# Projection weights' low parts moved to VectorE in halves, the next tile's rounding moved behind the ended tile's copies, and seven dummy matmuls added to the first norm

## The chip, the core and the metric

The program runs on one core of one Trainium2 chip. TensorE (PE) multiplies, VectorE (DVE) and ScalarE (ACT) do the work on rows, GpSimd (POOL) does some elementwise work and issues DMAs, and SyncE (SP) issues most loads. The metric is the device time in microseconds (us) of one execution, the median of several.

## What is computed

One layer of a transformer for 128 context tokens and 512 latent tokens, width 1024, in fp32. Cut to what matters here:

```python
h = rmsnorm(x, n1) * (1 + sc1) + sh1
aq, ak, av, bq, bk, bv, ga, gb = split(h @ w_in)      # 34 tiles of 128 columns
a_o = block_attention(aq, ak, av)                     # mixer A: 8 query heads, 2 key heads
b_o = neighbourhood_attention(bq, bk, bv, rel_bias)   # mixer B: 8 heads, window on the grid
m = sigmoid(ga) * (a_o @ w_br_a) + sigmoid(gb) * (b_o @ w_br_b)
x = x + g1 * (m @ w_out)
x = x + g2 * (square(relu(h2 @ w_mlp_in)) @ w_mlp_out)
y = rmsnorm(x, final_g)
```

The shifts, scales and gates come from `silu(c) @ w_mod + b_mod`.

## The kernel before

**Three products for one.** Every large product is made of three: an operand is split into a high part, rounded to the matmul's format, and a low part, what the rounding left off. PE adds high*high, high*low and low*high into one PSUM bank (`gemm_k`, lines 310 to 312). So each tile of weights needs a rounding on ACT (`wh`, line 263) and a subtraction `wl = wst - wh` (line 269 on POOL, line 271 on DVE), or, for the tiles in `LOSET`, a negated copy on ACT and a DMA that adds the weights to it (lines 265 and 266).

**The stages.** The first stage (0 to 52 us) makes the norm, the modulation and the first three tiles of the projection; its order is written out by hand (`manual_schedule`, from line 431), and `warm(n)` in it issues n dummy matmuls of 128x128 on PE. Then comes the attention (52 to 345 us): for mixer A and then mixer B, a head's scores (`S`, lines 672 and 725), softmax, transposes (`T`, lines 682 and 742), the split of the transposed rows into `ph` on ACT and `pl` on DVE (lines 620 and 621), and the product with the values into `po` (lines 689 and 690, 753 and 754). `combine` (lines 627 and 628) takes `po` away. Between these steps the Filler puts the matmuls of the remaining tiles of the projection on PE, 48 of them for one tile, two halves of 24, each half into a bank `pg`. In mixer A there is one `pg` bank, so the next half starts when the last half's copy (`raw`, `kr` or `qs`, lines 857 to 861 and 564, 565) has emptied it. After 345 us come the gates, the output projection and the MLP.

**Whose turn it is.** In the attention a scheduler orders each engine's instructions by the place at which the program issues them and by estimated times; each engine then runs its own row in order, and waits at the head of it. `fill_tile` (line 825) issues one tile's matmuls and copies. When a tile's last matmul is issued, `W.done()` (line 843) frees its weights and calls `conv` for the tile three places on: ACT's rounding in two halves, then the low part. The staging buffer `wst` (3 of them) is free for the next load on SP once the low part is made.

**Queries.** `a_q_rot` (line 817) turns a query tile by its position (`rope`: lines 554 to 557 on DVE), then `qa_part` splits it for the two heads e = 0 and 1: ACT copies (line 570), and a subtraction (line 571) on POOL or DVE by a bit of `QP`.

Of the kernel before, what the change touches and what calls it, by code (L numbers as in the profile page):

```python
# [19 lines left out]
KT = 8  # L20
EPS = 1e-6
FIRST = (4, 0, 5)
AFILL = (21, 29, 1, 10, 2, 6, 3, 14, 22)
BFILL = (30, 11, 7, 15, 12, 8, 16, 13, 9, 17)
# [3 lines left out]
WPO = 4  # L28
WP1 = 0
# [10 lines left out]
LAG = (0, 4)  # L40
MAN = (0,)
NSMALL = 348
QP = 3
Q0P = 0
RL = 1
OU = 1800
MG = 2
W2P = 2
WARM = (15, 1, 2, 5, 0, 2, 2)
NMS = 9  # L50
W0P = 0
WAH = (4, 6)
# [17 lines left out]
def trunk_layer(ctx: ExitStack, tc: tile.TileContext, xT, small_in, wmodA, wmodB, tabs, cacheK, cacheV, bias,  # L70
# [68 lines left out]
    def r32(ap):  # L139
        return ap.bitcast(F32)  # L140
# [94 lines left out]
    class Weights:  # L235
# [15 lines left out]
        def conv(self):  # L251
            self.feed()
            key, src = self.order[self.nc]
            self.busy -= 1
            st = self.st.pop(key)
            if key in EXTRA:
                self.extra = True
                hi, lo = (dp.tile([P, KT, P], F32R, tag="w4" + x, bufs=1, name="w4") for x in "hl")
            else:
                hi, lo = (wp.tile([P, KT, P], F32R, tag="w" + x, bufs=3, name="w" + x) for x in "hl")  # L260
                self.live += 2
            for ks in (slice(0, 4), slice(4, KT)) if key[0] == "in" else (slice(0, KT),):
                ACT.activation(hi[:, ks], st[:, ks], AF.Copy)  # L263
            if key in LOSET:
                ACT.activation(lo, r32(hi), AF.Copy, scale=-1.0)
                nc.gpsimd.dma_start(lo, src.bitcast(F32R).rearrange("p (k n) -> p k n", k=KT), accum_op=OP.add)
            elif key in WPOOLSET:
                for ks in (slice(0, 4), slice(4, KT)) if key[0] == "in" else (slice(0, KT),):
                    nc.gpsimd.tensor_sub(lo[:, ks], st[:, ks], r32(hi[:, ks]))  # L269
            else:  # L270
                DVE.tensor_sub(lo, st, r32(hi))
            self.t[self.nc] = (hi, lo)
            self.nc += 1

# [23 lines left out]
                OPS[0].ahead()  # L298

    OPS = []  # L300
    WPOOLSET = {("in", n) for n in AFILL + BFILL} | {("out", n) for n in range(WPO, KT)} | {("w1", n) for n in range(WP1)}
    EXTRA = {("out", 4), ("w1", 0)}
    LOSET = {(x, n) for x, a, b in LOACC for n in range(a, b) if x != "in" or n not in GATES[2:]}
    W = Weights()
# [50 lines left out]
    def mod_product(f, q):  # L355

        for k in range(4):
            g = 32 * k
            PE.matmul(pm[f % 2][g:g + 2, :256], sc_e[:, 4 * q + k], MS[f, q][:, k * 256:(k + 1) * 256],
                      start=q == 0, stop=q == 1, tile_position=(0, g))  # L360
# [70 lines left out]
    with tc.manual_schedule(engines={e.engine for e in (PE, ACT, DVE, nc.gpsimd, nc.sync)}):  # L431
        for f in range(2, KT):
            mod_load(f)
            if f % 2 == 0:
                w0_load(f // 2)
        for p in pm:
            DVE.memset(p[:, :256], 0.0)
        ACT.activation(sc_e, cc, AF.Exp, scale=-1.0)
        DVE.tensor_scalar(sc_e, sc_e, 1.0, None, op0=OP.add)
        DVE.reciprocal(sc_e, sc_e)  # L440
        DVE.tensor_mul(sc_e, sc_e, cc)
        DVE.tensor_scalar(b1, bm, 1.0, None, op0=OP.add)
        warm(WARM[0])
        for i in range(3):
            squares(i)
            warm(WARM[i + 1])
        mod_product(0, 0)
        squares(3)
        mod_product(0, 1)
        mod_rows(0, DVE)  # L450
        for h, sl in enumerate(HALVES):
            ACT.activation(rstd[:, sl], mean[h][:, :HT], AF.Ln, bias=eps)
        for h, sl in enumerate(HALVES):
            ACT.activation(rstd[:, sl], rstd[:, sl], AF.Exp, scale=-0.5)
        warm(WARM[4])
        mod_cols(0)
        warm(WARM[5])
        h_scaled(0)
        w0_conv(0, (0, 1), "h")
        w0_conv(0, (0,), "l")  # L460
        h_hi(0, SEG0)
        mod_product(1, 0)
        w0_conv(0, (2,), "h")
        w0_conv(0, (1, 2), "l")
        first_gemm(0, 0, 0)
        mod_product(1, 1)
        mod_rows(1)
        h_lo(0)
        first_gemm(0, 1, 0)
        mod_cols(1)  # L470
        h_scaled(1)
        first_gemm(0, 2, 0)
        h_hi(1)
        for i in range(3):
            first_gemm(0, i, 1)
        for q in range(2):
            mod_product(2, q)
        mod_rows(2)
        h_lo(1)
        w0_conv(1)  # L480
        for f in range(1, KT - 1):
            if f + 2 < KT:
                first_gemm(f, 0, 0)
            mod_cols(f + 1)
            h_scaled(f + 1)
            if f + 2 < KT:
                mod_product(f + 2, 0)
            else:
                first_gemm(f, 0, 0)
            first_gemm(f, 1, 0)  # L490
            if f + 2 < KT:
                mod_product(f + 2, 1)
            h_hi(f + 1)
            if f + 2 < KT:
                mod_rows(f + 2)
            first_gemm(f, 2, 0)
            for i in range(3):
                first_gemm(f, i, 1)
            h_lo(f + 1)
            if f % 2 == 0 and f < KT - 2:  # L500
                w0_conv(f // 2 + 1)
            if f == 3:
                silu_rows()
            if f in WAH:
                W.conv()
        for i in LASTO:
            for part in range(2):
                first_gemm(KT - 1, i, part)
# [316 lines left out]
    def fill_tile(n, F):  # L825
# [7 lines left out]
        for h in range(2):  # L833
            sl = HALVES[h]
            pg = ps_g()
            ps = pg[:, :HT]
            for k in range(KT):
                gemm_k(ps, w, H1, h, k, k, k == 0, k == KT - 1)
                if k == 3:
                    F.flush(1)  # L840
                yield UNIT
            if h == 1:
                W.done()
            if kind == "bq":
                if h == 0:
                    qs = [qs_tile() for _ in range(2)]
                for e in range(2):
                    q_part(qs[e], e, sl, ps)
            else:
                if h == 0:  # L850
                    raw = kr_tile() if kind == "bk" else o_tile("raw")
                    if kind == "bk":
                        for c in (P, 6 * P):
                            DQ[QO].dma_start(raw[:, c:c + P], cacheK[:, (j + 1) * P:(j + 2) * P])
                if kind == "bk":
                    lat = slice(max(sl.start, P), sl.stop)
                    if h == 0:
                        ACT.activation(raw[:, 0:P], ps[:, 0:P], AF.Copy)
                    ACT.activation(raw[:, lat.start + P:lat.stop + P], ps[:, lat.start - sl.start:], AF.Copy)
                else:  # L860
                    ACT.activation(raw[:, sl], ps, AF.Copy)
            F.flush(1)
            yield 0
        F.flush()
# [875 lines left out]
```

## Time and profile before

| | before |
|---|---|
| median of 3 runs | 943.21 us (939.26 to 946.52) |
| the profiled execution's own time | 939.48 us |
| its span, first to last instruction | 937.6 us |
| PE busy | 914.2 us (98%) |
| PE weight loads busy | 878.5 us (94%) |
| DVE busy | 700.8 us (75%) |
| ACT busy | 566.8 us (60%) |
| POOL busy | 242.4 us (26%) |

The profile shows one execution. Busy time of PE is modelled at its ends, so a stall shorter than a matmul's tail does not appear as idle time; the weight loads, which run just ahead, show it better. What counts is which wait ends last at the places where PE stands.

### The profile page before, as it was taken

To read this page: it belongs to the slowest core of one execution; us is meant where nothing else is said; L and a number is where in the kernel's file an instruction comes from. 1 tells how busy PE (TensorE), PEld (TensorE's weight loads), DVE (VectorE), ACT (ScalarE), POOL (GpSimd) and SP (SyncE) were. 2 spreads that over 40 slices of the span, in tenths; PEclk is the share of its full clock that TensorE was granted. 3 is DMA by queue.
4 is the path that set the end of the run, shared out by engine and by line. 5 is a ranking of instruction groups with operands and counts; after the bars stand their busy time and mean duration, and the time that the engine had idled before them with its cause. 6 is when DMAs were issued, how large, how long until landed. Compare 5 with 4: busy or idle time off the path is not lost.

```text
span 937.6 us, 16618 instructions
## 1 busy us (share of the span) xinstructions
PE 914.2 (98%) x6152; PEld 878.5 (94%) x6152; DVE 700.8 (75%) x1451; ACT 566.8 (60%) x1153; POOL 242.4 (26%) x260
## 2 busy tenths in 40 slices
PE   8999899999999999999999999999999999999996
PEld 6799789889999899999999999999999999999995
DVE  5774776756556788576778996986699768975898
ACT  3566677757656785675433667536763566447765
POOL 0042421314331011211120010444233532364130
PEclk9999999999999999999999999999999999999998
DMA  9783310026355379989743471888769877798573
GB/s 346 277 239 121 87 46 26 23 74 169 106 145 135 113 207 301 257 235 288 232 158 123 112 192 58 151 188 191 169 128 193 173 162 168 158 182 188 100 114 112
DMA packets 54033, 151.08 MB, mean 161 GB/s; under 512 B 6657, under 2 KB 10385, under 8 KB 53953
## 3 DMA queue, kind: packets, MB, share of 16 engines
q1 hardware_dynamic: 31440, 100.27, 32.5%
q0 software_dynamic: 21360, 48.45, 29.5%
q10 hardware_dynamic: 1152, 1.31, 0.4%
q8 instruction: 48, 0.79, 0.3%
q14 instruction: 33, 0.26, 0.1%
HBM read 138.72 MB, written 4.60 MB: 153 GB/s over the span
## 4 chain that ended last, share of the span: by engine, by line
PE 76%; DVE 10%; DMA 4%; issue 4%; ACT 4%; POOL 2%; SPq 0%; DVEq 0%; POOLq 0%; ACTq 0%
PE b L1609 9%; PE b L1610 9%; PE b L1608 9%; PE pg L310 6%; PE pg L312 6%; PE pg L311 6%; PE pss L312 3%; PE pss L311 3%; PE pss L310 3%; PE pt L312 2%; PE pt L311 2%; PE pt L310 2%; DMA wsb<-w 2%; PE pss L401 1%; PE pt L682 1%
## 5 line engine op out<-in xcount | busy, mean ns | idle before, releaser
L1355 ACT ACTIVATE wb<-wsb 128x512 fp32r<-128x512 f32 x140 | 87.1, 628 | 93.8 <-PE b L1610 60.9
L1609 PE MATMUL b<-op,wb 128*128 128x320 f32 x448 | 138.7, 310 | 1.0 <-DVE op L1424 1.0
L1608 PE MATMUL b<-op,wb 128*128 128x320 f32 x448 | 138.6, 309 | 0.2 <-ACT op L1423 0.2
L1610 PE MATMUL b<-op,wb 128*128 128x320 f32 x448 | 138.4, 309 | 0.0
L1356 DVE TENSOR_TENSOR wb<-wsb,wb 128x512 fp32r<-128x512 f32 x128 | 93.6, 735 | 32.3 <-ACT wb L1355 32.2
L1359 POOL DMA_DIRECT2D wsb<-w x84 | 73.5, 921 | 128.8 <-DVE wb L1356 95.0
L263 ACT ACTIVATE wh<-wst 128x512 fp32r<-128x512 f32 (+1 forms) x84 | 59.7, 737 | 46.1 <-PE pg L311 16.5
L1609 PEld LDWEIGHTS b<-op,wb 128*128 128x128 f32 x448 | 84.1, 188 | 1.8 <-DVE op L1424 1.8
L1608 PEld LDWEIGHTS b<-op,wb 128*128 128x128 f32 x448 | 84.1, 188 | 0.7 <-ACT op L1423 0.5
L1610 PEld LDWEIGHTS b<-op,wb 128*128 128x128 f32 x448 | 84.1, 188 | 0.0
L1063 DVE SCALAR_TENSOR_TENSOR mt<-wmt,cb 128x512 f32<-128x512 f32 x128 | 80.7, 687 | 4.5 <-DMA wmt<-wmodB 4.5
L269 POOL TENSOR_TENSOR wl<-wst,wh 128x512 fp32r<-128x512 f32 (+1 forms) x37 | 52.6, 1437 | 118.7 <-ACT wh L263 109.9
L621 DVE TENSOR_TENSOR pl<-pt,ph 128x512 fp32r<-128x512 f32 (+2 forms) x80 | 50.9, 636 | 35.1 <-ACT ph L620 30.5
L1340 POOL DMA_DIRECT2D wsb<-w x28 | 26.7, 954 | 138.3 <-DMA wsb<-w 43.1
L620 ACT ACTIVATE ph<-pt 128x512 fp32r<-128x512 f32 (+2 forms) x80 | 44.2, 553 | 21.8 <-PE pt L682 10.3
L1467 DVE SCALAR_TENSOR_TENSOR x<-b,parts,x 128x128 f32<-128x128 f32 (+1 forms) x116 | 46.8, 435 | 3.0 <-PE b L1610 2.2
L1608 PE MATMUL b<-t,wb 128*128 128x320 f32 x144 | 44.7, 310 | 0.5 <-DVE tp L1453 0.5
L1355 ACT ACTIVATE wb<-wst 128x512 fp32r<-128x512 f32 x56 | 34.8, 625 | 16.3 <-PE b L1610 9.7
L1610 PE MATMUL b<-t,wb 128*128 128x320 f32 x144 | 44.5, 309 | 0.0
L1609 PE MATMUL b<-t,wb 128*128 128x320 f32 x144 | 44.5, 309 | 0.0
L1424 DVE TENSOR_TENSOR op<-hid,op 128x1280 fp32r<-128x1280 f32 (+2 forms) x32 | 37.0, 1156 | 7.8 <-ACT op L1423 7.7
L1467 DVE SCALAR_TENSOR_TENSOR x<-tp,parts,x 128x320 f32<-128x320 f32 (+2 forms) x60 | 38.7, 673 | 1.0 <-ACT tp L1512 1.0
(874 smaller groups left out, 3037.4 us busy)
## 6 DMA issues: line engine op xcount, KB each, us to landing
wsb<-w POOLq DMA_DIRECT2D x112, 256.0 KB, 5.3
wst<-w SPq DMA_DIRECT2D x36, 512.0 KB, 4.0
wmt<-wmodB SPq DMA_DIRECT2D x32, 512.0 KB, 5.4
wst<-w_in SPq DMA_DIRECT2D x31, 512.0 KB, 4.1
wsb<-w SPq DMA_DIRECT2D x28, 512.0 KB, 4.2
ms<-wmodA SPq DMA_DIRECT2D x16, 512.0 KB, 8.0
wl<-w_in POOLq DMA_DIRECT2D x11, 512.0 KB, 8.2
bt<-bias SPq DMA_DIRECT2D x16, 320.0 KB, 6.1
```

The source lines that it names most:

```text
L263: ACT.activation(hi[:, ks], st[:, ks], AF.Copy)
L310: PE.matmul(ps, wh[:, k], xh[:, sl], start=first, stop=False)
L311: PE.matmul(ps, wh[:, k], xl[:, sl], start=False, stop=False)
L312: PE.matmul(ps, wl[:, k], xh[:, sl], start=False, stop=last)
L1063: DVE.scalar_tensor_tensor(t, st[:, q * 512:(q + 1) * 512], 1.0, r32(cb[2 * q + i][:, :512]), op0=OP.mult, op1=OP.mult, accum_out=parts[:, ...
L1355: ACT.activation(w[:, 0:4], t, AF.Copy)
L1356: (nc.gpsimd if o in BLKPOOL[l - 1] else DVE).tensor_sub(w[:, 4:8], t, r32(w[:, 0:4]))
L1359: nc.gpsimd.dma_start(t, self.src(l, c, n, e)[:, 4 * half:4 * half + 4], accum_op=OP.add)
L1467: DVE.scalar_tensor_tensor(X1[i][:, sl], src[:, sl.start - off:sl.stop - off], g[:, j:j + 1], X1[i][:, sl], op0=OP.mult, op1=OP.add)
L1608: PE.matmul(b, w[:, k], xh, start=not whole and k == 0, stop=False, skip_group_check=True)
L1609: PE.matmul(b, w[:, k], xl, start=False, stop=False, skip_group_check=True)
L1610: PE.matmul(b, w[:, 4 + k], xh, start=False, stop=o not in ("A11", "S2", "S1") and k == 3, skip_group_check=True)
```

## The change

Four edits. (1) `WPOOLSET` loses its tiles of the projection, so the 17 of them that are not in `LOSET` have `wl` made on DVE, in two halves of 128x512 each, instead of on POOL in the same halves; the three projection tiles that were on DVE already (18, 19 and 26) are made in halves too. (2) `QP` goes from 3 to 2: of the six `qa_part` subtractions of query tiles 1 to 3, the three for e = 0 go from POOL to DVE. (3) `W.done()` stands behind the copies of the tile that ended and no longer ahead of them. (4) `WARM` has two more dummies behind the first squares, two ahead of the first `mod_cols`, and three, with a new call, behind the product that follows the first `h_hi`.

```diff
-QP = 3
+QP = 2
-WARM = (15, 1, 2, 5, 0, 2, 2)
+WARM = (15, 3, 2, 5, 2, 2, 3)
@@ Weights.conv
             else:
-                DVE.tensor_sub(lo, st, r32(hi))
+                for ks in (slice(0, 4), slice(4, KT)) if key[0] == "in" else (slice(0, KT),):
+                    DVE.tensor_sub(lo[:, ks], st[:, ks], r32(hi[:, ks]))
@@
-    WPOOLSET = {("in", n) for n in AFILL + BFILL} | {("out", n) for n in range(WPO, KT)} | {("w1", n) for n in range(WP1)}
+    WPOOLSET = {("out", n) for n in range(WPO, KT)} | {("w1", n) for n in range(WP1)}
@@ first stage
         mod_product(1, 0)
+        warm(WARM[6])
         w0_conv(0, (2,), "h")
@@ fill_tile
                 yield UNIT
-            if h == 1:
-                W.done()
             if kind == "bq":
...
                     ACT.activation(raw[:, sl], ps, AF.Copy)
+            if h == 1:
+                W.done()
             F.flush(1)
```

The program of the change has its line numbers one or two higher from line 271 on. The first place is ACT's row where the tile that makes the first mixer-B key (`kr`) ends. Before:

```order
L620 ACTIVATE ph<-pt 128x512 x2
L263 ACTIVATE wh<-wst 128x512 x2
L787 ACTIVATE pc,cs<-pss,cm 128x128 x2
L620 ACTIVATE ph<-pt 128x512
L859 ACTIVATE kr<-pg 128x320
L570 ACTIVATE qs<-raw 64x640
L627 ACTIVATE ct<-po 64x512
```

The same place of the change:

```order
L622 ACTIVATE ph<-pt 128x512 x2
L263 ACTIVATE wh<-wst 128x512
L859 ACTIVATE kr<-pg 128x320
L789 ACTIVATE pc,cs<-pss,cm 128x128 x2
L622 ACTIVATE ph<-pt 128x512
L263 ACTIVATE wh<-wst 128x512
L581 ACTIVATE kh<-kr 128x896
L629 ACTIVATE ct<-po 64x512
```

The copy `kr` that empties `pg` has one rounding ahead of it and no longer two, a softmax pair and a split, and `ct`, with which `combine` empties `po`, no longer stands behind a query copy `qs`.

The second place is DVE's row at the same time: the turn of query tile 1 (`rot`, `raw`). Before:

```order
L785 TENSOR_REDUCE cm<-pss 128x2
L555 STREAM_SHUFFLE rot<-raw 128x512
L556 TENSOR_TENSOR rot<-rot,sin 128x512
L789 RECIPROCAL cr<-cs 128x2
L557 TENSOR_TENSOR raw<-rt,rot 128x512
L791 TENSOR_SCALAR pc<-pc,cr 128x128 x2
L621 TENSOR_TENSOR pl<-pt,ph 128x512
```

The same place of the change:

```order
L787 TENSOR_REDUCE cm<-pss 128x2
L557 STREAM_SHUFFLE rot<-raw 128x512
L272 TENSOR_TENSOR wl<-wst,wh 128x512
L791 RECIPROCAL cr<-cs 128x2
L558 TENSOR_TENSOR rot<-rot,sin 128x512
L793 TENSOR_SCALAR pc<-pc,cr 128x128 x2
L623 TENSOR_TENSOR pl<-pt,ph 128x512
L272 TENSOR_TENSOR wl<-wst,wh 128x512
L630 TENSOR_TENSOR ao_901<-po,ct 64x512
L559 TENSOR_TENSOR raw<-rt,rot 128x512
```

Two halves of `wl` stand in the row, each with a wait for ACT's `wh`, and `raw` stands behind both and behind `pl` and `ao`.

The third place is POOL's row at query tiles 2 and 3. Before:

```order
L269 TENSOR_TENSOR wl<-wst,wh 128x512 x4
L571 TENSOR_TENSOR qs<-raw,qs 64x640 x2
L269 TENSOR_TENSOR wl<-wst,wh 128x512 x2
L878 DMA bvT<-raw 128x128
L269 TENSOR_TENSOR wl<-wst,wh 128x512 x2
L571 TENSOR_TENSOR qs<-raw,qs 64x640 x2
```

The same place of the change:

```order
L592 DMA kl<-kl 64x896
L573 TENSOR_TENSOR qs<-raw,qs 64x640
L880 DMA bvT<-raw 128x128
L573 TENSOR_TENSOR qs<-raw,qs 64x640
```

Nothing is left on POOL between the two query splits but one DMA; the other half of each split is on DVE.

## Rows read from the trace of the kernel before

**Rows 1.** Busy time by stretch: length, PE, PEld, DVE, ACT, POOL, clock, DMA
```profile
62.00:200.00 138.00, 131.04 (x852) 120.29 (x851) 93.01 (x151) 93.29 (x209) 42.27 (x37) 1.00 0.25 74
200.00:345.00 145.00, 143.11 (x957) 135.34 (x956) 93.63 (x241) 96.17 (x229) 37.45 (x49) 1.00 0.49 135
```

**Rows 2.** What PE waited for from 62 to 345 us: total, times, longest
```profile
PE pg L310 <- DVE qs L565: 1.4, 1, 1.4
PE po L689 <- DVE ao L628: 1.4, 1, 1.4
PE pg L310 <- ACT kr L859: 1.3, 1, 1.3
PE pss L672 <- POOL qs L571: 1.0, 1, 1.0
...
PE pg L310 <- ACT raw L861: 0.3, 2, 0.2
```

**Rows 3.** Timeline, 96 to 103 us: start, length, engine, line, operation, idle before
```profile
96.48 1.15 ACT L263 ACTIVATE wh<-wst 128x512 fp32r<-128x512 f32 x2 [1.44 <-PE pg L311]
...
97.20 2.96 POOL L269 TENSOR_TENSOR wl<-wst,wh 128x512 fp32r<-128x512 f32 x2 [10.13 <-ACT wh L263]
...
97.35 1.67 DVE L556 TENSOR_TENSOR rot<-rot,sin 128x512 f32<-128x512 f32 x1
...
98.70 0.44 ACT L859 ACTIVATE kr<-pg 128x320 f32<-128x320 f32 x1
...
99.20 0.42 PE L310 MATMUL pg<-h0h,wh 128*128 128x320 f32 x1 [1.31 <-ACT kr L859]
...
100.74 0.74 ACT L570 ACTIVATE qs<-raw 64x640 fp32r<-64x640 f32 x1 [1.59 <-DVE raw L557]
...
101.50 0.59 ACT L627 ACTIVATE ct<-po 64x512 f32<-64x512 f32 x1
...
102.87 0.50 PE L689 MATMUL po<-ph,vst 128*128 128x512 f32 x1 [1.35 <-DVE ao L628]
```

**Rows 4.** Timeline, 168 to 174 us
```profile
168.60 3.33 POOL L269 TENSOR_TENSOR wl<-wst,wh 128x512 fp32r<-128x512 f32 x2 [8.16 <-ACT wh L263]
...
172.00 3.18 POOL L571 TENSOR_TENSOR qs<-raw,qs 64x640 fp32r<-64x640 f32 x2
...
173.60 0.41 PE L672 MATMUL pss<-kh,qs 128*128 128x320 f32 x1 [1.04 <-POOL qs L571]
```

**Rows 5.** Groups of POOL's instructions by line and shape: count, busy us, mean ns
```profile
L269 POOL TENSOR_TENSOR wl<-wst,wh 128x512 fp32r<-128x512 f32 x34 | 45.3, 1351 | 96.4 <-ACT wh L263 87.7 <-PE pt L682 8.7
...
L571 POOL TENSOR_TENSOR qs<-raw,qs 64x640 fp32r<-64x640 f32 x6 | 9.3, 1556 | 4.8 <-ACT qs L570 4.5
```

**Rows 6.** Groups of DVE's instructions by line and shape, 52 to 345 us
```profile
L556 DVE TENSOR_TENSOR rot<-rot,sin 128x512 f32<-128x512 f32 x5 | 5.0, 992 | 0.1
...
L557 DVE TENSOR_TENSOR raw<-rt,rot 128x512 f32<-128x512 f32 x4 | 4.7, 1170 | 0.1
...
L271 DVE TENSOR_TENSOR wl<-wst,wh 128x1024 fp32r<-128x1024 f32 x3 | 3.7, 1223 | 2.4 <-ACT wh L263 2.4
...
L554 DVE TENSOR_TENSOR rt<-kr,cos 128x512 f32<-128x512 f32 x1 | 2.3, 2319 | 0.0
...
L554 DVE TENSOR_TENSOR rt<-raw,cos 128x512 f32<-128x512 f32 x3 | 2.0, 680 | 0.0
L571 DVE TENSOR_TENSOR qs<-raw,qs 64x640 fp32r<-64x640 f32 x2 | 1.6, 820 | 0.1
```

**Rows 7.** Busy time by stretch in the first stage, columns as in the first group
```profile
16.00:19.20 3.20, 2.08 (x18) 1.33 (x18) 2.39 (x8) 2.44 (x7) 0.00 (x0) 1.00 1.02 399
19.20:22.80 3.60, 3.60 (x19) 2.34 (x19) 1.57 (x4) 0.84 (x3) 0.00 (x0) 0.53 1.05 393
```

**Rows 8.** Timeline of PE in the first stage
```profile
16.44 0.61 PE L372 MATMUL po<-pk,mrow 128*128 128x2 f32 x4 [0.55 <-DVE mrow L365]
16.91 0.69 PE L353 MATMUL pg<-ones 128*128 128x128 f32 x4
17.53 0.61 PE L359 MATMUL pt<-ms,sc_e 128*2 128x256 f32 x8
18.83 1.47 PE L401 MATMUL pss<-h0h,w 128*128 128x320 f32 x4 [0.68 <-ACT h0h L390]
```

## The prediction

> **What bounds the kernel now.** I read the page's first part, then the busy time by stretch, then PE's waits inside the attention, and last the timeline at the waits. PE is busy 98% of the span, so the change can only give back time in which PE stands or runs at a lower clock. All that it moves lies in two places: the first 25 us, and the attention from 52 to 345 us. In the attention PE is busy 131.04 of 138 us in the first part and 143.11 of 145 in the second [rows 1]: it stands 6.96 + 1.89 = 8.85 us. That is the ceiling of what edits 1 to 3 can give back as idle time; the weight loads show 17.71 + 9.66 us without a load, but many of those are the normal turns between kinds of matmul, so I count by the waits.
>
> PE's own waits there are few and single [rows 2]: 1.4 us for a query copy on DVE (`qs`, line 565), 1.4 for `ao`, with which DVE empties the output bank, 1.3 for ACT's `kr`, 1.0 for POOL's query split, 0.3 for ACT's `raw`. Two of them are seen at 96 to 103 us [rows 3]: ACT rounds the next tile in two halves (1.15 us) and does a softmax pair and a split before it copies `kr` at 98.70, and PE stands 1.31 us until 99.20 since there is one bank `pg`. In the same stretch POOL makes `wl` for 2.96 us, and DVE's `rot` beside it takes 1.67 us; the same kind of instruction without that company takes 0.68 [rows 6]. `rot` and `raw` being late makes ACT's `qs` late (100.74), `ct` stands behind it (101.50), and PE gets `po` at 102.87, 1.35 us late. The third is at 168 to 174 us [rows 4]: POOL makes two halves of `wl` for 3.33 us, and only then the query split that PE waits 1.04 us for.
>
> **Low parts on DVE.** Taken from POOL: 34 halves, 45.3 us, 1.35 each [rows 5]. Given to DVE: 34 halves. A whole one of 128x1024 takes 1.22 us on DVE, so a half at least 0.61, and an undisturbed instruction with the same shape takes 0.68 [rows 6]; I take 0.68, which makes 23.1 us. POOL's time was never on PE's path for its own sake, since the weights are rounded tiles ahead; it was only in the way, as above. What DVE gets back: `rot` 5 x (0.99 - 0.68) = 1.6 us, `raw` 4 x (1.17 - 0.68) = 2.0, `rt` of the key 2.32 - 0.68 = 1.6, in sum 5.2 us [rows 6]. The query halves of edit 2 add 3 x 0.82 = 2.5 us to DVE [rows 6] for 1.56 us each on POOL [rows 5]. So DVE gets 23.1 + 2.5 - 5.2 = 20.4 us more on 186.6 us of busy time between 62 and 345 us [rows 1], 11%; it goes from two thirds to three quarters of that stretch and does not become the bound.
>
> The Trainium skill has the same thing in "SBUF — State Buffer", section "Who interferes with whom": a DVE instruction with two SBUF inputs contends with a GpSimd instruction that reads SBUF, and the loser waits for the whole instruction. The 1.67 us of `rot` beside a POOL `wl`, against 0.68, agrees with it [rows 3, 6]. By that rule the three query splits that stay on POOL can still hold up a DVE instruction each, by up to 1.56 us, so that of the 5.2 us up to 4.7 could come back and the sum would have DVE at 25 us more; I keep the 5.2, since a split stands alone on POOL now.
>
> What this costs PE has no row. Below: if PE's waits for DVE (1.4 + 1.4 [rows 2]) only grow with DVE's load, 11% of 2.8 is 0.3 us. Above: if each of the 17 pairs holds up a `pl` or a maximum that PE waits for, by the pair's whole 1.36 us, 23 us. It is nearer to the low end, because PE already runs with DVE two thirds busy and waits for it 2.8 us in 283; but the pairs stand in the row between attention steps and the row is served in order, so I take five times the low end, **+1.5 us**. A DVE instruction of a pair that waits for ACT's `wh` holds up what is behind it: at the place shown, `cr`, `rot`, `pl`, `ao`, and so PE's `po`.
>
> **The query split.** At 168 to 174 us nothing of `wl` stands ahead on POOL, and the half that PE takes first is on DVE, 0.82 us behind ACT's copy and not 1.56 behind a 3.33 us pair. The wait of 1.0 goes: **-1.0**. If DVE's own `wl` pair is ahead of the turn `raw` there, the query is later by 1.36 us, less the 0.5 by which `raw` is faster, and a part stays; 0 to -1.0.
>
> **Rounding behind the copies.** `kr` has one rounding ahead instead of two, two softmax parts and a split; it can start about 97.1 and not 98.70, and the wait of 1.3 goes: **-1.3**. The two waits for `raw` (0.3) go too: **-0.3**. `ct` stands ahead of the query copy, so `ao` no longer waits for `rot` and `raw`: of 1.4 I take **-1.2**, since a key split and a rounding now stand ahead of `ct`. The 1.4 for the query copy on DVE (line 565) stays: in the change's row the second `qs` stands behind a pair of `wl`, 1.36 us, about what it waited. The rounding itself (ACT, 0.57 each) is only later by a copy or two, and its tile is three tiles from use, at some 14 us each (20 tiles in 283 us): nothing. DMAs: no issue is added. The next load on SP waits for the low part; that comes about as early as on POOL, 1.4 us of DVE for 2.5 to 3.3 of POOL, and the loads use a quarter of the DMA time there [rows 1]: nothing. POOL's DMAs for the stacked keys no longer stand behind a `wl`; PE has no wait for them in [rows 2]: nothing.
>
> **Dummies.** From 19.2 to 22.8 us the granted clock is 0.53, that is almost all at 1.2 GHz in place of 2.4, after a stretch in which PE was busy 2.08 of 3.20 us, while PE then works without a gap [rows 7]. Ahead of the drop PE stands 0.55 us for `mrow` and 0.68 for `h0h` [rows 8]. Two of the new dummies fall into the first gap and three into the second; four take 0.69 us including a tail [rows 8], so they fit, and the two early ones lie in a gap while DVE squares: cost nothing, and if a gap is shorter than they are, at most 7 x 0.17 = 1.2 us. What they can give back: 3.4 us at half clock hold 1.7 us of work at full clock, so at most 1.7; a part of that stretch is waiting of the sequencer, so I take **-1.4** if the clock then stays up, 0 if it doesn't. Five dummies are some 0.6 us of the 1.1 that PE stood; I think it a little likelier that the clock stays up.
>
> **Sum.** -1.3 - 0.3 - 1.2 - 1.0 + 1.5 - 1.4 = -3.7 us. On the profiled execution's 939.48 that is 935.8. That execution is 3.7 below the median of the runs (943.21) and next to their lowest; the four known executions average 942.1, and a median of new ones should lie about there, so I forecast 942.1 - 3.7 = 938.4 us.
>
> **Rivals.** (1) *The clock drops anyway.* Then the sum is -2.3: 939.8. For it: five short dummies against gaps of over half a microsecond. (2) *Most of the idle time goes.* If contention and order stand behind nearly all of PE's 8.85 us, and behind no new wait, -8.85 - 1.4 = -10.3: 931.8. Against it: a third of PE's idle time is behind steps that the change leaves alone or to which it puts a `wl` instead. (3) *DVE's row stalls; slower.* A half of `wl` at the head of DVE's row waits for ACT's `wh`, which in the change has a copy, a softmax pair and a split between its two halves; DVE's `pl` and `ao` wait behind it, and PE for those. The price is per tile: the gains are 5.2 us, so with 17 tiles it turns into a loss at 0.3 us each, and into one over 1% at (9.4 + 5.2) / 17 = 0.86 each. At 1.0 each the time is 942.1 + 17 - 5.2 = 953.9. Against it: at most places ACT's two halves stand near each other, and PE has two transposed banks in hand. The Trainium skill's "TensorE: Matmul & The Clock Gate", section "Part 1: The HAM clock gate", says that ACT and DVE serve their queues strictly in order, which this needs; the trace of before agrees with it in `ct` behind `qs` [rows 3].
>
> **How the numbers follow.** My forecast, from -7 to -3 us with the clock up, has 0.42; rival 1 has 0.20, and a DVE cost of two to four times what I took, which ends at about no change, 0.10 (938 to 945 both); rival 2 has 0.15; rival 3 has 0.13, of which 0.10 over 1%. A measurement of this kernel can tell about 1% (9.4 us) from no change: faster by over 1% needs under 932.7, which only rival 2 and a low draw of the runs reach, 0.15; slower by over 1% 0.10; within 0.75. The range leaves out the far half of rival 2 and all but the start of rival 3, with the runs' own scatter of 3 to 4 us in it: 930 to 948, and for the likeliest case alone 935 to 942.
>
> **What would show it.** Right: `rot` and `raw` on DVE at about 0.68 us; no PE wait for POOL's `qs` nor for `kr`; `wl` on DVE at 0.6 to 0.7, 34 times; the granted clock 1.00 from 6 us on; PE's idle time from 62 to 345 us down from 8.85 to about 6.5. Wrong: new waits of PE for `pl`, `nm` or `ao` of over 3 us in sum, DVE idle in front of `wl` for ACT's `wh` by more than 5 us, or a clock of about 0.5 in the first 25 us again.

## The result, and the profile after

| | before | changed |
|---|---|---|
| median, runs taken side by side | 942.61 us (937.72 to 946.52, 6 runs) | 933.39 us (930.98 to 934.15, 6 runs) |
| ratio to before, 95% interval | | 0.9918 [0.9892, 0.9944] |
| the same again, beside other experiments | 939.34 us (19 runs) | 931.56 us (930.64 to 932.30, 6 runs), 0.9910 [0.9890, 0.9930] |
| the profiled execution, its span | 939.48 us, 937.6 us | 933.35 us, 931.4 us |

The change gains 8 to 9 us, some 0.8 to 0.9%. The forecast was 938.4, with a range of 930 to 948: the time lies inside it, but 5 us below the forecast, near where rival 2 ("most of the idle time goes", 931.8) had put it. Besides, the executions of the changed kernel lie within 3 us of each other, those of before within 9.

Where the span's 6.2 us went, by the starts of PE's first matmul of each stage in the two profiles: 1.5 us are gained by 25 us (first matmul on `h1h` at 24.03, was 25.55); 0.5 is lost again before the first mixer-A scores (73.13, was 74.17; the run with the low parts moved alone loses 0.4 there); 5.3 are gained in mixer A (first mixer-B transposes at 210.70, was 217.01); 0.7 in mixer B; 1.7 are lost in the gates; and 0.9 come back in the MLP, which the change does not touch. The MLP alone, from its first matmul to its last, took between 350.3 and 353.2 us in the fourteen profiles of this study, so what differs there by under 3 us cannot be put down to the change.

Busy time by stretch after (length, PE, PEld, DVE, ACT, POOL, granted clock, DMA share, GB/s; to be read beside [rows 1] and [rows 7]):

```profile
62.00:200.00 138.00, 134.53 (x874) 123.51 (x873) 100.82 (x175) 96.33 (x215) 12.69 (x16) 1.00 0.26 75
200.00:345.00 145.00, 142.46 (x957) 135.47 (x956) 102.84 (x267) 98.16 (x234) 20.24 (x36) 1.00 0.53 143
```

```profile
16.00:19.20 3.20, 3.20 (x28) 2.41 (x27) 2.39 (x8) 2.44 (x8) 0.00 (x0) 1.00 1.02 398
19.20:22.80 3.60, 3.60 (x28) 2.90 (x29) 2.60 (x8) 1.07 (x4) 0.00 (x0) 1.00 1.05 395
```

In mixer A's stretch PE is busy 134.53 us and no longer 131.04: its idle time is halved (6.96 to 3.47). Counted over the same work, from the first mixer-A scores to the first mixer-B transposes, it falls from 7.70 to 3.25, and in mixer B from 1.15 to 0.66. In the second stretch it stands 2.54 instead of 1.89, and 1.9 of that is one wait in the gate stage. POOL does 33 us in place of 80, DVE 17 more (20.4 forecast). In the first stage the clock stays at 1.00, that is 2.4 GHz, where it was 0.53.

What PE waited for from 62 to 345 us after (total, times, longest), beside [rows 2]:

```profile
PE po L691 <- ACT ph L622: 2.4, 3, 1.0
PE pg L313 <- DMA wl<-w_in: 1.9, 1, 1.9
PE pss L727 <- DVE vst L615: 0.5, 1, 0.5
PE po L692 <- DVE pl L623: 0.3, 1, 0.3
PE pt L684 <- DVE pl L623: 0.3, 1, 0.3
PE pg L311 <- ACT raw L861: 0.2, 1, 0.2
```

The waits of before for `kr`, `ao`, POOL's `qs` and, unforeseen, DVE's `qs` are gone. No wait for DVE has taken their place. ACT's split `ph` is what ends last now (2.4 us, 0.7 before).

Groups of DVE's instructions from 52 to 345 us after (count, busy us, mean ns, idle before and for whom), beside [rows 6]:

```profile
L272 DVE TENSOR_TENSOR wl<-wst,wh 128x512 fp32r<-128x512 f32 x39 | 26.3, 686 | 11.1 <-ACT wh L263 10.7
L573 DVE TENSOR_TENSOR qs<-raw,qs 64x640 fp32r<-64x640 f32 x5 | 4.1, 820 | 1.5 <-ACT qs L572 1.4
L558 DVE TENSOR_TENSOR rot<-rot,sin 128x512 f32<-128x512 f32 x5 | 3.4, 678 | 0.0
L559 DVE TENSOR_TENSOR raw<-rt,rot 128x512 f32<-128x512 f32 x4 | 2.7, 678 | 0.0
L556 DVE TENSOR_TENSOR rt<-kr,cos 128x512 f32<-128x512 f32 x1 | 0.7, 693 | 0.0
```

The halves of `wl` take 0.686 us, `rot` and `raw` 0.678 (0.992 and 1.170 before), the key's `rt` 0.693 (2.319 before): the durations of the prediction are met to a hundredth or so.

And the place of [rows 3] after (timeline: start, length, engine, line, operation, idle before):

```profile
95.12 0.42 ACT L859 ACTIVATE kr<-pg 128x320 f32<-128x320 f32 x1
...
96.35 0.67 DVE L558 TENSOR_TENSOR rot<-rot,sin 128x512 f32<-128x512 f32 x1
...
97.33 0.68 DVE L623 TENSOR_TENSOR pl<-pt,ph 128x512 fp32r<-128x512 f32 x1
97.93 0.68 DVE L272 TENSOR_TENSOR wl<-wst,wh 128x512 fp32r<-128x512 f32 x1
98.11 0.59 ACT L629 ACTIVATE ct<-po 64x512 f32<-64x512 f32 x1
...
98.73 0.68 DVE L630 TENSOR_TENSOR ao<-po,ct 64x512 f32<-64x512 f32 x1
...
100.54 1.48 ACT L572 ACTIVATE qs<-raw 64x640 fp32r<-64x640 f32 x2
...
102.05 0.60 ACT L622 ACTIVATE ph<-pt 128x512 fp32r<-128x512 f32 x1
...
102.69 0.50 PE L691 MATMUL po<-ph,vst 128*128 128x512 f32 x1 [1.00 <-ACT ph L622]
```

`kr` starts at 95.12, right behind one rounding, and `ct` at 98.11 comes ahead of the query copies; PE misses neither. Instead both query copies of 1.48 us stand ahead of a `ph`, and PE waits 1.00 for that: of 2.66 us at this place 1.00 is left.

### The profile page after: what moved, and what is told of

Same layout as the page of the kernel before. It is cut to its first block, busy times and chain, and to the rows that moved or that the text cites. A ratio compares the mean times of both kernels' runs of the same rounds, so it can differ in the third digit from the quotient of the medians.

```text
span 931.4 us, 16637 instructions
## 1 busy us (share of the span) xinstructions
PE 913.3 (98%) x6166; PEld 879.2 (94%) x6166; DVE 716.2 (77%) x1491; ACT 566.5 (61%) x1153; POOL 193.3 (21%) x223
## 3 DMA queue, kind: packets, MB, share of 16 engines
q10 hardware_dynamic: 1152, 1.31, 0.4%
## 4 chain that ended last, share of the span: by engine, by line
PE 75%; DVE 8%; issue 6%; DMA 5%; ACT 3%; POOL 1%; SPq 0%; DVEq 0%; POOLq 0%; ACTq 0%
PE b L1611 10%; PE b L1612 10%; PE b L1610 10%; PE pg L311 6%; PE pg L313 6%; PE pg L312 6%; PE pss L313 3%; PE pss L311 3%; PE pss L312 3%; DMA wl<-w_in 2%; PE pt L313 2%; PE pt L311 2%; PE pt L312 2%; PE pt L684 2%; PE pss L402 1%
## 5 line engine op out<-in xcount | busy, mean ns | idle before, releaser
L272 DVE TENSOR_TENSOR wl<-wst,wh 128x512 fp32r<-128x512 f32 (+1 forms) x51 | 40.4, 802 | 16.9 <-ACT wh L263 16.4
```

## The experiments

All times are medians; the ratio is to the kernel before, run side by side on the same chip, with a 95% interval. Three chips were used, one for each group, so ratios are compared between groups, not times. The ratio is close to one of means, while the differences in the text are of medians within a group, so the two need not agree to a tenth of a per cent: for the first four rows the ratios give 1.8, 2.8, 1.5 and 1.3 us.

| kernel | us | before | ratio |
|---|---|---|---|
| before, dummies alone | 938.77 | 939.91 | 0.9981 [0.9964, 0.9997] |
| before, rounding behind the copies alone | 937.32 | 939.91 | 0.9970 [0.9953, 0.9986] |
| before, low parts on DVE alone | 938.91 | 939.91 | 0.9984 [0.9970, 0.9999] |
| before, query split alone | 939.13 | 939.91 | 0.9986 [0.9967, 1.0006] |
| changed kernel | 931.56 | 939.34 | 0.9910 [0.9890, 0.9930] |
| changed, low parts back on POOL | 936.99 | 939.34 | 0.9971 [0.9956, 0.9986] |
| changed, rounding ahead again | 934.70 | 939.34 | 0.9946 [0.9927, 0.9965] |
| changed, old dummies | 934.67 | 939.34 | 0.9945 [0.9923, 0.9966] |
| changed, POOL busy with copies of the low parts | 943.60 | 941.07 | 1.0028 [1.0009, 1.0047] |
| changed, low parts whole | 932.75 | 941.07 | 0.9915 [0.9890, 0.9940] |
| changed, all query splits on POOL | 933.94 | 941.07 | 0.9926 [0.9901, 0.9951] |
| changed, two more low parts on DVE | 931.67 | 941.07 | 0.9897 [0.9868, 0.9926] |

### One edit at a time

Dummies alone:

```diff
-WARM = (15, 1, 2, 5, 0, 2, 2)
+WARM = (15, 3, 2, 5, 2, 2, 3)
+        warm(WARM[6])
```

> The kernel before with the seven dummies alone. My theory (the clock's dip at 19.3 to 22.7 us is what the dummies take away, and the rest of the 6.2 us of span lies in mixer A): clock 1.00 from about 5 us on, the first gemm of the second half at about 24.0 us instead of 25.55, everything after it as before; span 1.5 us shorter, time -1.5 us (941). Rival, the steadier clock start also removes the scatter of the runs (before 937.7 to 946.5, after 931.0 to 934.2): then the median goes down by 4 to 5 us and the runs lie within 3 us. Rival, the dummies do nothing alone: clock at half again near 19 us, no change.

Measured: -1.1 us. The clock stays at 1.00 and the first matmul on `h1h` starts at 24.25, 1.30 us earlier; the waits in the attention are those of before, one by one. The rival that this edit also takes the scatter away falls: the runs still lie within 4.4 us. In 7 of its 12 runs the mean granted clock is 0.995, in 4 it is 0.997, and those 7 take 939.4 us on average, the 4 take 937.5. A lower mean clock need not be a fall that costs time, though: in all fourteen profiles the clock also falls behind PE's last matmul, and in the run with the rounding ahead (below) that alone makes a mean of 0.996 (PE ends at 924.0 us; the clock is 0.50 from 926 to 932).

Rounding behind the copies alone:

```diff
-            if h == 1:
-                W.done()
             if kind == "bq":
...
+            if h == 1:
+                W.done()
             F.flush(1)
```

> The kernel before with the rounding of the next tile behind the ended tile's copies alone (low parts still on the third engine, GpSimd). My prediction had 2.8 us from this edit (kr 1.3, raw 0.3, ao 1.2). Theory A (the order on ScalarE carries most of mixer A's 5.3 us): 3 to 5 us shorter, rot still 1.0 to 1.7 us beside a low part on GpSimd, the waits for kr and raw gone. Theory B (contention of GpSimd with VectorE carries most): at most 1.5 us shorter, since rot and raw stay slow and ao late; the wait for kr goes and another takes its place.

Measured: -2.6 us, which is between the two theories' figures. Its waits from 52 to 345 us say why (the first three rows):

```profile
PE pt L682 <- DVE pl L621: 1.9, 2, 1.6
PE pss L672 <- POOL qs L571: 1.5, 2, 1.0
PE po L689 <- DVE ao L628: 0.9, 1, 0.9
```

The waits for `kr` (1.31) and for DVE's query copy near 137 us (1.44) are gone, but near 100 us PE now waits 1.6 for DVE's `pl` and 0.9 for `ao`: 2.5 us at a place where 2.66 stood before. At this place, moving the rounding alone only hands the wait on to DVE, which is slow there beside POOL: `rot` takes 1.68 us, the pair of `pc` 1.50, and `kl` ahead of `ao` 2.23 (1.07 in the changed kernel).

Low parts on DVE alone:

```diff
-                DVE.tensor_sub(lo, st, r32(hi))
+                for ks in (slice(0, 4), slice(4, KT)) if key[0] == "in" else (slice(0, KT),):
+                    DVE.tensor_sub(lo[:, ks], st[:, ks], r32(hi[:, ks]))
...
-    WPOOLSET = {("in", n) for n in AFILL + BFILL} | {("out", n) for n in range(WPO, KT)} | {("w1", n) for n in range(WP1)}
+    WPOOLSET = {("out", n) for n in range(WPO, KT)} | {("w1", n) for n in range(WP1)}
```

> The kernel before with the low parts on VectorE in halves alone (rounding still ahead of the copies, both query halves on GpSimd). Theory B (contention carries most of mixer A's gain): 3 to 5 us shorter, rot and raw 0.68 us each, the wait for ao gone, the wait for kr of 1.3 us still there. Theory A (order on ScalarE carries it): about 1 us either way, the low parts' waits for ScalarE's rounding cost what contention gave back. My prediction's price for VectorE's longer row, 1.5 us, would show as new waits of TensorE for pl, ao or nm of about that sum.

Measured: -1.0 us, theory A's figure, but not for its reason. `rot` and `raw` take 0.681 us and the wait for `ao` is gone, as theory B said; what hides the gain is that ACT's order keeps the wait for `kr`, and that the wait near 133 us grows: 0.63 for `ph` and 1.61 for DVE's `qs`, where before has 0.21 and 1.44. The pair of `wl`, behind ACT's two roundings, stands there ahead of the first `qs`. PE's waits from 52 to 345 us:

```profile
PE pg L311 <- DVE qs L566: 1.6, 1, 1.6
PE pg L311 <- ACT kr L860: 1.3, 1, 1.3
PE po L690 <- ACT ph L621: 1.1, 2, 0.6
PE pg L311 <- DVE vst L614: 0.9, 2, 0.4
```

And its profile shows something that before's does not. Busy time by stretch (columns as above) for this kernel, and then for before:

```profile
132.00:139.00 7.00, 4.76 (x22) 4.21 (x21) 5.20 (x10) 3.70 (x7) 2.13 (x2) 0.76 0.24 75
```

```profile
132.00:139.00 7.00, 5.22 (x31) 4.01 (x30) 6.71 (x12) 5.22 (x11) 2.53 (x2) 1.00 0.18 72
```

Behind PE's waits for `ph` (0.63) and `qs` (1.61) the granted clock falls to 1.2 GHz, 0.76 on the mean of these 7 us. Two rows of PE in that kernel show the price:

```profile
136.03 0.47 PE L313 MATMUL pg<-h0h,wl 128*128 128x320 f32 x1
136.30 0.47 PE L311 MATMUL pg<-h1h,wh 128*128 128x320 f32 x1
```

The matmuls start 0.27 us apart and not 0.15 as at full clock, from 135.36 to 138.16 us, eleven of them: 11 x 0.12 = 1.3 us. That comes on top of the wait itself.

Query split alone:

```diff
-QP = 3
+QP = 2
```

> The kernel before with the three e = 0 query splits on VectorE alone. Prediction: the wait of 1.0 us for GpSimd's qs at 173 us goes, nothing else moves: -1.0 us (941.6), not to be told from no change by the time, but by the waits. Rival: the split on VectorE then waits behind other work there and the wait moves to another place: 0.

Measured: -0.8 us, an interval that reaches to no change. The wait for POOL's `qs` is gone and no other has come, as predicted. Its profiled execution, 941.47 us, shows both falls of the clock, the first one twice as long as in before (the first matmul on `h1h` at 26.94 instead of 25.55), the second from 138 to 142 us.

In sum the four edits alone give 1.1 + 2.6 + 1.0 + 0.8 = 5.5 us by the medians, and together 7.8 on the chip of the second group. By the ratios it is 7.4 against some 8.5, with 1.4 to 1.9 us of uncertainty either way on each, so it is not shown that the whole is more than the sum.

### One edit taken back

> The changed kernel again, unaltered, in the same rounds as the next three, as their base. If the gain is that of the whole (9.2 us by the medians so far), 931 to 933 us at 940 for before. The four single edits give 1.1, 2.6, 1.0 and 0.8 us, in sum 5.5: if they simply add, about 934.5. If the runs of before scatter because the granted clock falls a second time near 135 us in some of them, then no run here has a mean clock under 0.997 and they lie within 4 us.

Measured: 931.56, 7.8 us below before, and not the 934.5 of a plain sum. Its six runs have mean clocks of 0.996 to 0.998 and lie within 1.7 us. Two of them have 0.996, under the 0.997 that was expected at least; since the clock also falls behind PE's last matmul, that does not tell of a fall near 135 us.

Low parts back on POOL (the diff of the low parts above, reversed):

> The changed kernel with the low parts back on GpSimd. If the edits add: +1.0 us, what this edit gave alone. If contention of GpSimd and VectorE counts once the order on ScalarE no longer hides it: +2.5 to +3, with TensorE's waits for pl (1.9 in the run with the copies first alone) and ao (0.9) back, and rot at 1.0 to 1.7 us. If VectorE's longer row costs what my prediction put it at (1.5 us), this kernel gets that back and is no slower.

Measured: +5.4 us, nearly twice the largest figure expected. The timeline near 100 us:

```profile
94.94 1.68 DVE L557 TENSOR_TENSOR rot<-rot,sin 128x512 f32<-128x512 f32 x1
...
96.82 1.67 POOL L269 TENSOR_TENSOR wl<-wst,wh 128x512 fp32r<-128x512 f32 x1 [0.74 <-ACT wh L263]
...
97.27 1.50 DVE L792 TENSOR_SCALAR pc<-pc,cr 128x128 f32<-128x128 f32 x2
98.69 0.68 DVE L622 TENSOR_TENSOR pl<-pt,ph 128x512 fp32r<-128x512 f32 x1
...
99.42 0.66 PE L683 MATMUL pt<-pk,pa 128*128 128x128 f32 x4 [1.60 <-DVE pl L622]
```

`rot` takes 1.68 us beside one half of `wl`, the pair of `pc` 1.50 beside the other; after the change they take 0.67 and 0.48. Those 2.0 us stand ahead of `pl` in DVE's row, and PE waits 1.60 for it. Near 133 us PE waits 1.05 for `ph` and 1.13 for DVE's `qs`, and the clock falls behind that (0.76 from 132 to 139 us). The wait for `ao` that was expected back did not come. In the profile mixer A takes 4.7 us more than in the changed kernel's second one, of which the fall is some 1.3 by the rows of the same fall above; mixer B takes 1.2 more.

Rounding ahead again (the diff of the rounding, reversed):

> The changed kernel with the rounding ahead of the copies again. If the edits add: +2.6. If this edit also takes away the gap at 135 us after which the clock falls in some executions: +4 to +5, with the waits for kr (1.3) and for VectorE's qs (1.4 to 1.6) back, and a mean clock of 0.995 in some of the runs in spite of the dummies.

Measured: +3.1 us. `kr` (1.3) and `qs` (1.6) are waited for again; the mean clock is 0.995 in 2 of 7 runs, although this profile's clock does not fall (1.00 from 132 to 139 us behind the same waits).

Old dummies (the diff of `WARM`, reversed):

> The changed kernel with the dummies of before. The first gemm of the second half at 25.3 us instead of 24.0, and the rest shifted by as much: +1.3 to +1.9 us, clock about 0.5 from 19 to 22.7 us. In executions in which the fall lasts twice as long, as it did in one profile (19 to 26 us), +3; then the median +2.

Measured: +3.1 us, more than the 1.3 to 1.9 expected. In this profile the clock stays up without the new dummies: 1.00 from 19.2 to 22.8 us, the first matmul on `h1h` at 24.13. So the fall is not certain. The seven runs are of two kinds: three with a mean clock of 0.994 to 0.995 take 935.5 to 937.0 us, four with 0.997 or 0.998 take 932.5 to 934.7. The step between the two is 2.5 us on average. That it is the fall near 19 us is likely but not shown, since no profile of this kernel has one. That the better four still lie 2 us above the changed kernel is not explained by the clock; in the profile it is the gates (a wait of 1.95 for a DMA where the changed kernel's second profile has 0.58) and the MLP (2.6 us).

### Is it the contention?

The changed kernel, with POOL subtracting as well, into a buffer that nobody reads:

```diff
+                if key[0] == "in" and key[1] in AFILL + BFILL:
+                    scr = wp.tile([P, 4, 120], F32R, tag="scr", bufs=1, name="scr")
+                    for ks in (slice(0, 4), slice(4, KT)):
+                        nc.gpsimd.tensor_sub(scr, st[:, ks, :120], r32(hi[:, ks, :120]))
```

> The changed kernel, with GpSimd doing the 16 or so tiles' low parts once more, in halves of 128x480 into a scratch buffer that nobody reads, while VectorE does the real ones as in the changed kernel. VectorE's and ScalarE's rows keep their order but for a few instructions. If contention is what taking the low parts off GpSimd removes (5.4 us inside the whole change): rot, pc and pl take 1.0 to 1.7 us again where a scratch subtraction lies beside them, and the time is 4 us or more above the changed kernel (936 or more). If instead it was GpSimd's low parts coming late, or the order of VectorE's row: within 1 us of the changed kernel (931 to 933).

Measured: 1.0028 against 0.9910, 1.2% or 11 us slower than the changed kernel, and slower than before. The place near 100 us, and below it groups of DVE and POOL from 52 to 330 us:

```profile
96.12 1.28 DVE L562 TENSOR_TENSOR rot<-rot,sin 128x512 f32<-128x512 f32 x1
...
97.16 1.31 POOL L276 TENSOR_TENSOR scr<-wst,wh 128x480 fp32r<-128x480 f32 x1 [0.31 <-ACT wh L263]
...
97.32 1.43 DVE L797 TENSOR_SCALAR pc<-pc,cr 128x128 f32<-128x128 f32 x2
...
98.67 0.68 DVE L627 TENSOR_TENSOR pl<-pt,ph 128x512 fp32r<-128x512 f32 x1
...
99.40 0.66 PE L688 MATMUL pt<-pk,pa 128*128 128x128 f32 x4 [1.44 <-DVE pl L627]
```

```profile
L272 DVE TENSOR_TENSOR wl<-wst,wh 128x512 fp32r<-128x512 f32 x37 | 37.7, 1031 | 11.3 <-PE pss L732 7.0 <-ACT wh L263 3.9 <-PE pss L679 0.2
L797 DVE TENSOR_SCALAR pc<-pc,cr 128x128 f32<-128x128 f32 x16 | 4.8, 347 | 0.2
L562 DVE TENSOR_TENSOR rot<-rot,sin 128x512 f32<-128x512 f32 x5 | 4.0, 797 | 0.0
L627 DVE TENSOR_TENSOR pl<-pt,ph 128x512 fp32r<-128x512 f32 x56 | 38.3, 686 | 11.1 <-ACT ph L626 8.4 <-PE po L695 2.1
...
L276 POOL TENSOR_TENSOR scr<-wst,wh 128x480 fp32r<-128x480 f32 x34 | 51.9, 1527 | 97.1 <-issue 88.8 <-ACT wh L263 6.2 <-POOL rt L560 1.0
```

Near 100 us the work that nobody reads brings back the wait that the run with the low parts on POOL has there: `rot` takes 1.28 us, the pair of `pc` 1.43, and PE waits 1.44 for the `pl` behind them. `wl` on DVE goes from 0.686 to 1.031 us and `pc` from 0.284 to 0.347 on the mean; `pl`, which takes one of its inputs from PSUM, stays at 0.686; the expectation had `pl` slow too, and that was wrong. PE waits 6.1 us for `pl` in six places, 1.4 for `nm` and 1.5 for `qs`. No engine waits for the result of POOL's subtractions, so late low parts are ruled out as the reason of the time, and contention by itself makes the wait near 100 us. The size does not carry over to the change. Of what DVE loses here, 37 x 0.345 = 12.8 us is on its own `wl`, which meets POOL's scratch work on the same tiles and was not on DVE when POOL made the low parts. And SP's loads wait 13.9 us for `scr` to leave the staging buffer, though no wait of PE for a load follows from 52 to 330 us. The Trainium skill's "SBUF — State Buffer", section "Who interferes with whom", names the DVE instructions with two SBUF inputs and `tensor_scalar` as those that can collide with POOL; `wl`, `rot` and `pc` on the one side and `pl` on the other agree with it.

### Halves, the query split, and a try at more

Low parts on DVE in one piece:

```diff
-                for ks in (slice(0, 4), slice(4, KT)) if key[0] == "in" else (slice(0, KT),):
-                    DVE.tensor_sub(lo[:, ks], st[:, ks], r32(hi[:, ks]))
+                DVE.tensor_sub(lo, st, r32(hi))
```

> The changed kernel with each low part on VectorE in one piece of 128x1024 (1.22 us) and not in two halves. Rival 3 of the prediction (a low part that waits for ScalarE's rounding holds up VectorE's row) would show here first, since the piece waits for both roundings: +2 us or more, with waits of TensorE for pl, qs or ao. If VectorE's row has slack where the low parts stand: within 1 us.

Measured: 0.9915 against 0.9910, no difference that can be told. Near 100 us PE waits 0.24 and no longer 1.00; near 132 us the wait for `qs` is back (1.37), with the fall of the clock behind it, and one of 0.9 for `pl` is new. The halves help at one place and hurt at the other. Waits of the kind that rival 3 names do appear, then, with a piece twice as long, but the time does not show its 2 us or more.

All query splits on POOL (`QP = 3`):

> The changed kernel with all six query splits of tiles 1 to 3 on GpSimd. Prediction: the wait of 1.0 us for GpSimd's split near 170 us is back: +1.0. If without low parts ahead of it on GpSimd the split comes early enough, the wait is at most 0.7 (as in the run with the low parts on VectorE alone) and the time the same within 1 us.

Measured: 0.9926 against 0.9910, some 1.5 us, inside the intervals, so the time tells nothing. POOL's `qs` is waited for twice, 1.8 us in sum, where the prediction had 1.0.

Tiles 23 and 27 of the projection on DVE:

```diff
-LOACC = (("in", 21, 22), ("in", 29, 30), ("in", 20, 26), ("in", 27, 34), ("br", 0, 8))
+LOACC = (("in", 21, 22), ("in", 29, 30), ("in", 20, 23), ("in", 24, 26), ("in", 28, 34), ("br", 0, 8))
```

> An attempt at a faster kernel: the changed kernel with the low parts of projection tiles 23 and 27 made on VectorE and no longer by a DMA that adds. The wait of TensorE for that DMA at 343 us (1.9 and 0.6 us in two profiles of the changed kernel) and the one near 392 us (up to 0.5) go: -1 to -2 us. If VectorE's two pieces hold up osl or mt there, that is given back: 0.

Measured: 0.9897, not to be told from the changed kernel. From 335 to 400 us PE waits for nothing any more, so both waits are gone, but one of 1.05 for the next such DMA appears at 413 us. Taking two tiles out of the chain of adding DMAs moves the wait to a later one of them.

## Why the prediction was right or wrong

**Right.** What bounds the kernel (PE, so only its gaps count), the direction, and nearly every line of the list of signs: durations on DVE, no wait for `kr` or POOL's `qs`, the clock at 1.00. That PE's idle time from 62 to 345 us is 6.0 where 6.5 was forecast is luck: the 1.5 that the forecast had for DVE did not come, and 1.9 of the 6.0 is a wait for a DMA that it did not have; in the changed kernel's second profile the idle time is 5.0. The 4.7 us that the prediction allowed for the three splits left on POOL did not come either (`rot` and `raw` 0.678, the splits on DVE 0.820). And the time lies in the range because the range takes in rival 2: the gain is 7.8 to 9.2 us by the medians, more than twice the 3.7 of the sum. By the terms of the sum:

- *`kr` -1.3, `ao` -1.2*: these waits went. What the sum left out is the work that moved in: `ph` behind two query copies, 1.0 near 100 us and 0.9 near 132. And `ao` was put down to ACT's order alone; the run with the rounding moved alone still has 0.9 of it, the run with the low parts moved alone has none. So POOL's company had a part in it.
- *`raw` -0.3*: it did not go. PE waits 0.2 us for `raw` in the one profile of the changed kernel, 0.5 in the other.
- *POOL's query split -1.0*: right by the waits, in the run with that edit alone and in the one without it; neither time can be told from no change.
- *Dummies -1.4*: right for one execution in which the clock falls (1.30 and 1.52 measured). But the fall comes in four of the five profiles with the old dummies and in none of the nine with the new.

**Wrong: the term for DVE, +1.5.** It priced the 34 halves as a longer row, and what DVE gets back (5.2 us) only as busy time. The runs show the opposite sign: inside the whole change, taking the low parts off POOL is worth 5.4 us, alone 1.0. The step that failed is the one that priced POOL's company by DVE's busy time and not by what stands behind the slow instruction in DVE's row. One `rot` of 1.68 us and a pair `pc` of 1.50 delay a `pl` by 2.0, and PE waits for it. DVE's longer row has no wait of PE of its own in the changed kernel; with the rounding ahead of the copies it has one, the 0.6 us more near 133. The term's low end was also read too low: PE's waits for DVE in before are 4.0 us from 62 to 345, not 2.8, since those for `vst`, `pl` and `nm` (1.2 in sum) were left out. The sign that was to speak against the forecast, DVE idle ahead of `wl` for ACT's `wh` by over 5 us, did come true (10.7 us, longest 4.2) and shows in no wait of PE.

**Wrong: "the 1.4 for the query copy stays".** It went. In before ACT's two roundings stand ahead of its first query copy there (134.37) and DVE's `rot`, 1.24 us beside POOL's pair, ahead of the second `qs`; in the change the first copy has no rounding ahead of it, and the pair of `wl` only takes the place of the turn. The second `qs` is behind the pair, as the prediction said, but PE is held 0.9 us by `ph` and comes to the bank later. And the wait stood for more than 1.4. Eight of the fourteen profiles have one of 1.1 to 1.6 us for DVE's `qs` between 131 and 139 us, and in five of these the clock falls behind it, at 1.3 us more; in none of the six without the wait does it fall there. The profile of before was one of the three that were spared, so no row of it could show this price.

**Not in the sum: the gates.** The wait of 1.9 us for a DMA that adds to `wl` has no term. The same wait is 0.6 in the changed kernel's second profile, 0.7 with the dummies alone, and 0.2 to 2.0 in the others that have it; before has none at that place. In part it may be the change's, since PE comes there 7 us earlier; but the two profiles of the changed kernel come there within 0.4 us of each other and differ by 1.3, so it goes by when that DMA lands as well.

**Why the low parts are worth more inside the change than alone.** The difference is clear of the intervals: a ratio of 0.9984 [0.9970, 0.9999] alone, and 0.9971 against 0.9910 when they are taken back. The profiles show two reasons, and a place that is none. Near 100 us PE waited in before for `kr` (1.31) and `ao` (1.35). With ACT's order mended alone, PE comes earlier to the late `pl` (1.59) and still waits for `ao` (0.92); with POOL out of the way alone, the wait for `kr` stays (1.26); with both, 1.0 for `ph` is left. Here taking POOL away is worth 1.4 us alone and 1.5 on top of the other edit, which is the same. Near 133 us it differs in sign: the low parts on DVE alone make PE's wait there longer, from 1.65 to 2.24, and only with the rounding behind the copies does it come down to 0.9. The second reason is the clock. Its fall behind that wait is in the profile with the low parts alone and in the one with them taken back, at some 1.3 us. By the length of mixer A (first scores to first mixer-B transposes) the low parts alone save 1.3 us and taking them back costs 4.7; without the two falls it is an estimated 2.6 and 3.4. The prediction added the two edits as if they were independent; near 133 us they are not.

**The 3 us between span and median.** The medians of the first comparison differ by 9.2 us, the two profiles by 6.1. The runs of before explain part: of 70 with a mean clock in its usual range, the 18 below 0.995 have a median of 942.85 us, the 27 at 0.995 one of 940.12, the 25 above it 938.84. The profiles with the old dummies show none, one or two falls of the clock that PE pays for, the two of the changed kernel none. How much of the 3 us that is, and how much the chips differ (the medians of before are 939.3 to 942.6 over the four groups of runs), stays open.

**Rivals.** Rival 2 came about in size, but its reason only in part: over the same work, PE's idle time in the attention falls from 8.85 us to 3.9, not to nothing. The rest of the 7.8 to 9.2 us is the first stage (1.5) and what the last paragraph leaves open, so that rival 2's figure was met is partly luck. Rival 1 did not come about in any of the nine profiles with the new dummies; but without them the clock does not always fall either, so the dummies do not save their 1.4 in each execution. Rival 3 does not show in the time.

## What to carry to other kernels

Where an engine's slow instruction is slow because of its neighbour, price it by what stands behind it in the row and who waits for that, not by its extra busy time; a run that repeats the neighbour's work into a spare buffer measures it. Where an engine waits for one thing, ask what it would wait for next if it came there earlier: without the 1.3 us for `kr`, PE stood 1.6 for a `pl` that was late all along. And of a wait of over a microsecond in PE's row look at several profiles, since the clock may fall behind it in some executions and not in the one that was profiled.

## What the runs showed of the hardware

- The granted clock falls behind the same wait in some executions and not in others. It does in 5 of the 8 profiles with the wait for `qs`, at some 1.3 us, and near 19 us in 4 of the 5 with the old dummies. There the first matmul on `h1h` starts at 25.10, 25.26 and 25.55, and once at 26.94, against 24.13 in the one that was spared. That this makes part of the scatter of before is likely; how much is not shown.
- The mean clock of an execution also holds a fall behind PE's last matmul, in all fourteen profiles, so that a mean of 0.996 comes with a fall that PE pays for (low parts in one piece) and without one (rounding ahead).
- DVE instructions with both inputs in SBUF were slow beside POOL's elementwise work: `rot` 1.68 us and not 0.68, `kl` 2.23 and not 1.07, the key's `rt` 2.32 and not 0.69; a pair of 128x128 scalings took 1.50 and not 0.48. `pl` and `ao`, which read PSUM, took 0.68 to 0.69 in each kernel.
- Open: the MLP, the same in all kernels, took 352.0 to 353.2 us in the five profiles with the old dummies, 350.3 to 351.5 in eight of the nine with the new, and 352.2 in the ninth. ACT's rounding there waits for weight loads that land at other moments. No run here shows whether seven matmuls at 17 us can move that, or whether it is chance.
